# Batch normalization over 256 channels: half tiles in six buffers in place of whole tiles in three

## The chip, the cores and the metric

The kernel runs on one core of one Trainium2 chip. The metric is the time of one execution on the device, in microseconds; less is better. A DMA here is a transfer between the chip's main memory (DRAM) and the core's on-chip memory of 128 partitions. The core has 16 DMA engines; the SP engine issues the loads on one hardware queue, the ScalarE (ACT) engine the stores on another, and every transfer of 128 rows is spread over all 16 DMA engines.

## The reference

The input x has 32 images of 256 channels of 128 x 128 numbers (float32, 537 MB). Every channel gets one scale and one shift:

```
mean = running_mean.reshape(1, -1, 1, 1)
var = running_var.reshape(1, -1, 1, 1)
gamma = gamma.reshape(1, -1, 1, 1)
beta = beta.reshape(1, -1, 1, 1)
return gamma * (x - mean) / np.sqrt(var + eps) + beta
```

Each number is read once, gets a multiplication and an addition, and is written once: 1074 MB in both directions.

## The kernel before

A tile is one image and one block of 128 channels: 128 partitions by 16,384 columns (`HW`), 8 MB. There are 64 of them (`NT`), taken in `order`: all images of the first channel block, then of the second. Three buffers `t0` to `t2` are used in turn; the work is done in place.

SP issues the loads. Ahead of everything it issues half of tile 0 (L87), the four parameter rows (L90), the other half of tile 0 (L94) and tiles 1 and 2 (L96), with no wait between the tiles. After that, load i (L103) waits for two things: that store i-3 has emptied its buffer (L102), and that VectorE (DVE) has done the first part of tile i-1, which it does as soon as load i-1 has landed (L104, the semaphore `vdone`). So one load is in flight at a time.

DVE works out scale and shift per channel (L106 to L124), and then does two instructions a tile (`vector_part`, L127): columns 0 to `STEP` (2560), then `STEP` to `VCOLS` (14,336), or to `VLAST` (9216) in the last tile. Tile 0 is cut at its middle instead, since it is loaded in two halves. ACT does the rest of the columns (`scalar_part`, L138) once both DVE parts are done, and waits there for the store of tile i-1 to have landed (L164); then it issues the store of tile i (L153). So one store is in flight at a time. In the last tile ACT waits for neither DVE nor the store before, and only its store waits for both parts.

`loaded{s}` and `stored{s}` are semaphores for each buffer; a transfer adds 16, one from each DMA engine. There is no scheduler: each engine runs its instructions in the order that the code writes them.

Of the kernel before, what the change touches and what calls it, by code (L numbers as in the profile page):

```python
# [6 lines left out]


NBUF = 3
PAD = 936  # L10


STEP = 2560
VCOLS = 14336
VLAST = 9216


@with_exitstack
def kernel(
    ctx: ExitStack,  # L20
    tc: tile.TileContext,
    x: bass.AP,
    gamma: bass.AP,
    beta: bass.AP,
    running_mean: bass.AP,
    running_var: bass.AP,
    out: bass.AP,
):
    nc = tc.nc
    eps = 1e-5  # L30
    f32 = mybir.dt.float32

    N, C, H, W = x.shape
    P = nc.NUM_PARTITIONS
    assert C % P == 0
    NCB = C // P
    HW = H * W
    NT = N * NCB
    B = 32
    NQ = P // B  # L40
    NE = 16
    NPAR = 4

    xr = x.rearrange("n (cb p) h w -> (n cb) p (h w)", p=P)
    outr = out.rearrange("n (cb p) h w -> (n cb) p (h w)", p=P)

    def tile_of(name, *shape):
        return nc.alloc_sbuf_tensor(name, list(shape), f32)

    rows = tile_of("rows", B, NPAR * C)  # L50
    turned = tile_of("turned", B, NPAR * C)
    par = tile_of("par", P, NPAR, NCB)
    eps_t = tile_of("eps_t", P, 1)
    std_t = tile_of("std_t", P, NCB)
    rstd_t = tile_of("rstd_t", P, NCB)
    scale_t = tile_of("scale_t", P, NCB)
    ms_t = tile_of("ms_t", P, NCB)
    shift_t = tile_of("shift_t", P, NCB)
    tile_of("pad", P, PAD)
    bufs = [tile_of(f"t{s}", P, HW) for s in range(NBUF)]  # L60

    names = [f"loaded{s}" for s in range(NBUF)] + [f"stored{s}" for s in range(NBUF)]
    names += ["early", "vdone", "adone", "fetched", "vec", "act"]
    sems = {name: nc.alloc_semaphore(name) for name in names}
    loaded = [sems[f"loaded{s}"] for s in range(NBUF)]
    stored = [sems[f"stored{s}"] for s in range(NBUF)]
    early, vdone, adone, fetched, vec, act = (sems[n] for n in names[2 * NBUF :])
    used = range(min(s.num for s in sems.values()), max(s.num for s in sems.values()) + 1)
    assert len(used) == len(sems)

    count = [0]

    def step(inst, sem=None, value=None):
        if sem is not None:
            inst._wait_ge(sem, value)
        elif count[0]:
            inst._wait_ge(vec, count[0])
        inst.then_inc(vec, 1)
        count[0] += 1
        return count[0]  # L80

    left, right = slice(0, HW // 2), slice(HW // 2, HW)
    last = NT - 1
    order = [n * NCB + cb for cb in range(NCB) for n in range(N)]

    with tc.tile_critical():  # L86
        nc.sync.dma_start(out=bufs[0][:, left], in_=xr[order[0]][:, left]).then_inc(early, 16)  # L87
        zeroed = step(nc.vector.memset(rows[:], 0.0))  # L88
        for r, ap in enumerate((running_var, gamma, beta, running_mean)):
            inst = nc.sync.dma_start(out=rows[0:NE, r * C : (r + 1) * C], in_=ap.partition_broadcast(NE))  # L90
            if r == 0:
                inst._wait_ge(vec, zeroed)
            inst.then_inc(fetched, 16)
        nc.sync.dma_start(out=bufs[0][:, right], in_=xr[order[0]][:, right]).then_inc(loaded[0], 16)  # L94
        for i in range(1, NBUF):
            nc.sync.dma_start(out=bufs[i][:], in_=xr[order[i]]).then_inc(loaded[i], 16)  # L96
    tc.close()
    tc.compile()  # L98

    for i in range(NBUF, NT):  # L100
        s, turn = i % NBUF, i // NBUF
        nc.sync.wait_ge(stored[s], 16 * turn)  # L102
        inst = nc.sync.dma_start(out=bufs[s][:], in_=xr[order[i]]).then_inc(loaded[s], 16)  # L103
        inst._wait_ge(vdone, 2 * (i - 1) + 1)  # L104

    step(nc.vector.memset(eps_t[:], eps))  # L106
    step(nc.vector.transpose(out=turned[:], in_=rows[:]), fetched, 16 * NPAR)  # L107

    blocks = turned[:].rearrange("p (rc q b) -> p rc q b", q=NQ, b=B)
    flat = par[:].rearrange("p r cb -> p (r cb)")  # L110
    for q in range(NQ):
        placed = step(nc.vector.tensor_copy(out=flat[q * B : (q + 1) * B], in_=blocks[:, :, q, 0]))  # L112
    var_t, gamma_t, beta_t, mean_t = (par[:, r] for r in range(NPAR))
    nc.scalar.activation(  # L114
        out=std_t[:],
        in_=var_t,
        func=mybir.ActivationFunctionType.Sqrt,
        bias=eps_t[:],
        scale=1.0,
    )._wait_ge(vec, placed).then_inc(act, 1)  # L120
    step(nc.vector.reciprocal(out=rstd_t[:], in_=std_t[:]), act, 1)  # L121
    step(nc.vector.tensor_mul(out=scale_t[:], in0=gamma_t, in1=rstd_t[:]))  # L122
    step(nc.vector.tensor_mul(out=ms_t[:], in0=mean_t, in1=scale_t[:]))  # L123
    ready = step(nc.vector.tensor_sub(out=shift_t[:], in0=beta_t, in1=ms_t[:]))  # L124
    nc.vector.wait_ge(vec, ready)

    def vector_part(i, first, end):  # L127
        t, cb = bufs[i % NBUF], order[i] % NCB
        return nc.vector.tensor_scalar(  # L129
            out=t[:, first:end],  # L130
            in0=t[:, first:end],
            scalar1=scale_t[:, cb : cb + 1],
            scalar2=shift_t[:, cb : cb + 1],
            op0=mybir.AluOpType.mult,
            op1=mybir.AluOpType.add,
        ).then_inc(vdone, 1)

    def scalar_part(i, first):  # L138
        t, cb = bufs[i % NBUF], order[i] % NCB
        return nc.scalar.activation(  # L140
            out=t[:, first:],
            in_=t[:, first:],
            func=mybir.ActivationFunctionType.Identity,
            bias=shift_t[:, cb : cb + 1],
            scale=scale_t[:, cb : cb + 1],
        ).then_inc(adone, 1)

    def landed(i):
        return loaded[i % NBUF], 16 * (i // NBUF + 1)

    def store(i):
        s = i % NBUF
        nc.scalar.dma_start(out=outr[order[i]], in_=bufs[s][:])._wait_ge(adone, i + 1).then_inc(stored[s], 16)  # L153

    vector_part(0, 0, HW // 2)._wait_ge(early, 16)
    vector_part(0, HW // 2, VCOLS)._wait_ge(*landed(0))
    for i in range(1, NT):
        vector_part(i, 0, STEP)._wait_ge(*landed(i))
        vector_part(i, STEP, VLAST if i == last else VCOLS)
    for i in range(last):  # L160
        nc.scalar.wait_ge(vdone, 2 * (i + 1))
        inst = scalar_part(i, VCOLS)
        if i:
            inst._wait_ge(stored[(i - 1) % NBUF], 16 * ((i - 1) // NBUF + 1))  # L164
        store(i)
    scalar_part(last, VLAST)._wait_ge(*landed(last))
    nc.scalar.wait_ge(vdone, 2 * NT)
    store(last)

    for s in range(NBUF):  # L170
        nc.sync.wait_ge(stored[s], 16 * ((NT - s + NBUF - 1) // NBUF))
    nc.sync.sem_clear(used)
# [30 lines left out]
```

## Time and profile before

| | |
|---|---|
| Time, median of 3 runs | 2481.03 us (2480.61 to 2481.18) |
| The profiled execution | 2480.81 us, span 2479.5 us |
| Moved | 1073.85 MB, mean 433 GB/s |
| Load of 8 MB, issue to landing (median) | 37.0 us |
| Store of 8 MB, issue to landing (median) | 36.5 us |
| DVE `tensor_scalar`, all | 505.2 us in 128 instructions |
| ACT `activation` on tiles, all | 138.2 us in 64 instructions |

A line of the timeline has the start in the span, the duration, the engine and line, the operation with its tiles and shapes, and in brackets how long the engine was idle before it and what ended that. A line of the waits has the waiting engine and line, what it waited for, the total in us, how many times, and the longest. A line on a DMA queue has its packets, its MB, and the time of its packets as a share of 16 engines' span. The row of digits is the span in 40 equal slices, in tenths of busy time. SPq and ACTq are the parts of SP and ACT that issue transfers.

### The profile page before, as it was taken

To read this page: it belongs to the slowest core of one execution; us is meant where nothing else is said; L and a number is where in the kernel's file an instruction comes from. 1 tells how busy PE (TensorE), PEld (TensorE's weight loads), DVE (VectorE), ACT (ScalarE), POOL (GpSimd) and SP (SyncE) were. 2 spreads that over 40 slices of the span, in tenths; PEclk is the share of its full clock that TensorE was granted. 3 is DMA by queue.
4 is the path that set the end of the run, shared out by engine and by line. 5 is a ranking of instruction groups with operands and counts; after the bars stand their busy time and mean duration, and the time that the engine had idled before them with its cause. 6 is when DMAs were issued, how large, how long until landed. Compare 5 with 4: busy or idle time off the path is not lost.

```text
span 2479.5 us, 514 instructions
## 1 busy us (share of the span) xinstructions
DVE 508.7 (21%) x139; ACT 139.8 (6%) x66; POOL 0.2 (0%) x4
## 2 busy tenths in 40 slices
DVE  2122121221212212122121221212212122121220
ACT  0000000000000000000000000000000000000001
POOL 0000000000000000000000000000000000000000
DMA  9999999999999999999999999999999999999999
GB/s 412 435 438 427 437 438 429 436 438 429 435 438 430 435 439 430 433 438 433 431 438 432 432 438 432 432 438 432 432 438 433 431 438 433 431 438 435 430 438 410
DMA packets 18708, 1073.85 MB, mean 433 GB/s; under 512 B 2128, under 2 KB 2192, under 8 KB 2192
## 3 DMA queue, kind: packets, MB, share of 16 engines
q1 hardware_dynamic: 9488, 536.94, 50.1%
q10 hardware_dynamic: 9216, 536.88, 50.0%
q14 instruction: 4, 0.03, 0.0%
HBM read 536.94 MB, written 536.87 MB: 433 GB/s over the span
## 4 chain that ended last, share of the span: by engine, by line
DMA 92%; DVE 4%; another core or an unknown queue 2%; ACT 0%; issue 0%; SPq 0%; DVEq 0%
DMA t<-in_x_dram 92%; DVE t L129 4%; ACT t L140 0%; SPq L90 0%; DVE rows L88 0%; DVEq L98 0%; SPq L86 0%
## 5 line engine op out<-in xcount | busy, mean ns | idle before, releaser
L129 DVE TENSOR_SCALAR t<-t,scale_t,shift_t 128x11776 f32<-128x11776 f32 (+2 forms) x128 | 505.2, 3989 | 1928.4 <-DMA t<-in_x_dram 1928.3
L140 ACT ACTIVATE t<-t,shift_t,scale_t 128x2048 f32<-128x2048 f32 x64 | 138.2, 2159 | 2297.3 <-DMA out_dram<-t 2274.5
L107 DVE STREAM_TRANSPOSE turned<-rows 32x1024 f32<-32x1024 f32 x1 | 1.2, 1232 | 7.6 <-DMA rows<-in_running_mean_dram 7.6
L114 ACT ACT_TABLE_LOAD x1 | 1.3, 1283 | 6.4 <-PEq L98 6.4
L88 DVE MEMSET rows<- 32x1024 f32 x1 | 0.9, 912 | 1.2 <-SPq L86 1.2
L106 DVE MEMSET eps_t<- 128x1 f32 x1 | 0.1, 59 | 4.4 <-PEq L98 4.4
L114 ACT ACTIVATE std_t<-par,eps_t 128x2 f32<-128x2 f32 x1 | 0.3, 295 | 8.5 <-DVE par L112 8.5
L112 DVE COPY par<-turned 32x8 f32<-32x8 f32 x4 | 0.7, 162 | 0.1
L121 DVE RECIPROCAL rstd_t<-std_t 128x2 f32<-128x2 f32 x1 | 0.2, 165 | 0.4 <-ACT std_t L114 0.4
L122 DVE TENSOR_TENSOR scale_t<-par,rstd_t 128x2 f32<-128x2 f32 x1 | 0.2, 161 | 0.0
L123 DVE TENSOR_TENSOR ms_t<-par,scale_t 128x2 f32<-128x2 f32 x1 | 0.2, 161 | 0.0
L124 DVE TENSOR_TENSOR shift_t<-par,ms_t 128x2 f32<-128x2 f32 x1 | 0.2, 160 | 0.0
L187 POOL MEMSET const-bfloat16-1.0<- 128x1 bf16 x1 | 0.1, 101 | 0.0
L187 POOL MEMSET const-uint8-127<- 128x1 uint8 x1 | 0.1, 101 | 0.0
L187 POOL MEMSET const-float32-0.0<- 128x1 f32 x1 | 0.1, 98 | 0.2 <-issue 0.2
L187 POOL MEMSET const-float32-1.0<- 128x1 f32 x1 | 0.1, 98 | 0.0
## 6 DMA issues: line engine op xcount, KB each, us to landing
t<-in_x_dram SPq DMA_DIRECT2D x2, 4096.0 KB, 16.0
out_dram<-t ACTq DMA_DIRECT2D x64, 36.5
t<-in_x_dram SPq DMA_DIRECT2D x63, 37.0
rows<-in_running_var_dram SPq DMA_DIRECT2D x1, 16.0 KB, 11.2
rows<-in_gamma_dram SPq DMA_DIRECT2D x1, 16.0 KB, 11.0
rows<-in_beta_dram SPq DMA_DIRECT2D x1, 16.0 KB, 10.7
rows<-in_running_mean_dram SPq DMA_DIRECT2D x1, 16.0 KB, 10.7
```

Of the source, the lines that this page charges most:

```text
L88: zeroed = step(nc.vector.memset(rows[:], 0.0))
L106: step(nc.vector.memset(eps_t[:], eps))
L107: step(nc.vector.transpose(out=turned[:], in_=rows[:]), fetched, 16 * NPAR)
L112: placed = step(nc.vector.tensor_copy(out=flat[q * B : (q + 1) * B], in_=blocks[:, :, q, 0]))
L114: nc.scalar.activation(out=std_t[:], in_=var_t, func=mybir.ActivationFunctionType.Sqrt, bias=eps_t[:], scale=1.0,)._wait_ge(vec, placed).t ...
L121: step(nc.vector.reciprocal(out=rstd_t[:], in_=std_t[:]), act, 1)
L122: step(nc.vector.tensor_mul(out=scale_t[:], in0=gamma_t, in1=rstd_t[:]))
L123: step(nc.vector.tensor_mul(out=ms_t[:], in0=mean_t, in1=scale_t[:]))
L124: ready = step(nc.vector.tensor_sub(out=shift_t[:], in0=beta_t, in1=ms_t[:]))
L129: return nc.vector.tensor_scalar(out=t[:, first:end], in0=t[:, first:end], scalar1=scale_t[:, cb : cb + 1], scalar2=shift_t[:, cb : cb + 1 ...
L140: return nc.scalar.activation(out=t[:, first:], in_=t[:, first:], func=mybir.ActivationFunctionType.Identity, bias=shift_t[:, cb : cb + 1] ...
L187: nc = _bacc.Bacc("TRN2", target_bir_lowering=False, num_devices=1)
```

## The change

Each tile is cut into two halves by columns (`SPLIT = 2`), and each half is a tile of its own, 128 x 8192, 4 MB, with its own load, its own work and its own store. There are 128 of them, and six buffers of half the size, so the on-chip memory used is the same. `VCOLS` and `VLAST` are halved; `STEP` stays at 2560. The rules of waiting are the same lines with the new index: load i waits for store i-6 and for the first DVE part of half tile i-1; ACT's part of half tile i waits for the store of half tile i-1. Six loads are issued without a wait between them at the start, the first of them ahead of the parameter rows. The special cut of tile 0 and its semaphore `early` go, since a half tile is what it was cut into. The two halves of one image and block follow each other, so the rows of a transfer are 32,768 bytes out of 65,536.

```
-NBUF = 3
+SPLIT = 2
+NBUF = 3 * SPLIT
...
-VCOLS = 14336
-VLAST = 9216
+VCOLS = 7168
+VLAST = 4608
...
+    COLS = HW // SPLIT
+    NT = N * NCB * SPLIT
...
-    bufs = [tile_of(f"t{s}", P, HW) for s in range(NBUF)]
+    bufs = [tile_of(f"t{s}", P, COLS) for s in range(NBUF)]
...
-    order = [n * NCB + cb for cb in range(NCB) for n in range(N)]
+    order = [(n, cb, h) for cb in range(NCB) for n in range(N) for h in range(SPLIT)]
+
+    def part_of(ap, i):
+        n, cb, h = order[i]
+        return ap[n * NCB + cb][:, h * COLS : (h + 1) * COLS]
+
+    def load(i):
+        s = i % NBUF
+        return nc.sync.dma_start(out=bufs[s][:], in_=part_of(xr, i)).then_inc(loaded[s], 16)
...
-        nc.sync.dma_start(out=bufs[0][:, left], in_=xr[order[0]][:, left]).then_inc(early, 16)
+        load(0)
...
-        nc.sync.dma_start(out=bufs[0][:, right], in_=xr[order[0]][:, right]).then_inc(loaded[0], 16)
         for i in range(1, NBUF):
-            nc.sync.dma_start(out=bufs[i][:], in_=xr[order[i]]).then_inc(loaded[i], 16)
+            load(i)
...
     for i in range(NBUF, NT):
-        s, turn = i % NBUF, i // NBUF
-        nc.sync.wait_ge(stored[s], 16 * turn)
-        inst = nc.sync.dma_start(out=bufs[s][:], in_=xr[order[i]]).then_inc(loaded[s], 16)
-        inst._wait_ge(vdone, 2 * (i - 1) + 1)
+        s = i % NBUF
+        nc.sync.wait_ge(stored[s], 16 * (i // NBUF))
+        load(i)._wait_ge(vdone, 2 * (i - 1) + 1)
...
     def store(i):
         s = i % NBUF
-        nc.scalar.dma_start(out=outr[order[i]], in_=bufs[s][:])._wait_ge(adone, i + 1).then_inc(stored[s], 16)
+        nc.scalar.dma_start(out=part_of(outr, i), in_=bufs[s][:])._wait_ge(adone, i + 1).then_inc(stored[s], 16)
 
-    vector_part(0, 0, HW // 2)._wait_ge(early, 16)
-    vector_part(0, HW // 2, VCOLS)._wait_ge(*landed(0))
-    for i in range(1, NT):
+    for i in range(NT):
         vector_part(i, 0, STEP)._wait_ge(*landed(i))
         vector_part(i, STEP, VLAST if i == last else VCOLS)
```

## The prediction

> **What bounds the kernel now.** I read the page first (engines, DMA, chain), then the waits, then the middle of the chain and of the timeline, then the packet records of the trace.
>
> ```profile
> DVE 508.7 (21%) x139; ACT 139.8 (6%) x66; POOL 0.2 (0%) x4
> DMA  9999999999999999999999999999999999999999
> q1 hardware_dynamic: 9488, 536.94, 50.1%
> q10 hardware_dynamic: 9216, 536.88, 50.0%
> DMA 92%; DVE 4%; another core or an unknown queue 2%; ACT 0%; issue 0%; SPq 0%; DVEq 0%
> ```
> The engines compute a quarter of the time, the DMA engines are busy in every slice. Queue 1 is the loads, queue 10 the stores: 9216 packets are 64 stores of 144, namely 128 rows of 65,536 bytes and 16 four-byte marks that count up the semaphore, so each of the 16 DMA engines moves 8 rows a store.
>
> ```profile
> SPq L102 <- DMA out_dram<-t: 1395.0, 61, 66.0
> SPq L103 <- DVE t L129: 984.8, 61, 16.5
> ...
> ACT t L140 <- DMA out_dram<-t: 2274.5, 62, 43.3
> ```
> A load waits last (16.1 us a time) for vector work on the load before it; a store waits for the store before it (36.7 us through its ACT part). Neither queue ever holds a second transfer in the steady part.
>
> ```profile
> 1208.96 7.93 DVE L129 TENSOR_SCALAR t<-t,scale_t,shift_t 128x2560 f32<-128x2560 f32 x2 [30.70 <-DMA t<-in_x_dram]
> 1210.59 77.61 SPq L103 DMA_DIRECT2D t<-in_x_dram  x3
> 1233.09 2.09 ACT L140 ACTIVATE t<-t,shift_t,scale_t 128x2048 f32<-128x2048 f32 x1 [36.57 <-DMA out_dram<-t]
> 1235.21 0.34 ACTq L153 DMA_DIRECT2D out_dram<-t  x1
> 1247.60 7.93 DVE L129 TENSOR_SCALAR t<-t,scale_t,shift_t 128x2560 f32<-128x2560 f32 x2 [30.71 <-DMA t<-in_x_dram]
> ```
> One tile takes 38.64 us (1208.96 to 1247.60). A load lands, DVE does 2560 columns, the next load is issued 1.63 us later; half a period on, a store lands, ACT does 2048 columns, the next store is issued 2.12 us later. The chain of waits counts those 1.62 us of DVE, but the DMA engines do not stop there. In the packet records 65,536-byte packets follow each other every 2.4141 us on each engine, 16 of them and two marks make the 38.64 us, and no engine has an idle microsecond from 1.95 us to its end at 2476.6 to 2479.0. So the bound is bytes: 64 loads and 64 stores of 8 rows are 1024 packets per engine, 2472 us.
>
> The order of packets matters for the change. On the engine that finishes last, a period reads (L load, S store, dot a mark) `L . L L L S L S . S S S L S L S L`: two transfers take turns, and while one queue is empty the other runs alone for 4 packets (5 or 6 on engines that are ahead). From the mark of a load to the next load being ready at the engines is 3.03 us: 0.35 to landing, 0.03, 1.62 of DVE, 0.04, and about 1.0 from issue (also the 1.0 between the first issue at 0.95 us and the first packet at 1.95). A newly ready queue is taken one whole packet late, and a mark costs its queue a turn. For stores the same sum with 2.09 us of ACT is 3.5 us.
>
> **The change, part by part.** Tiles of 8192 columns, 128 loads and 128 stores, six buffers.
>
> (1) Rows of 32,768 bytes. Only the first tile has such packets now. Seven steps of one engine there, between 14 and 22 us, take 8.466 us, so 1.2094 each, 2.4189 a pair against 2.4141: 4.7 ns on 1016 rows per engine = **+4.8 us**. They are loads running alone; mixed with stores they are not seen. With 65,536 bytes loads and stores cost the same, alone or mixed, so I take the load's price; the ends are 0 (half of 2.4141) and, for a loss, twice it, 9.6.
>
> (2) Marks: 256 transfers in place of 129, 6 ns each on the path: **+0.8 us**.
>
> (3) DVE and ACT. Per half tile DVE does 2560 columns (1.62) and 4608: the 8192- and 6144-column rows (4.55 and 3.48) give 0.52 ns a column and 0.27 fixed, so 2.7 us; ACT does 1024 columns: 2048 took 2.09 and 7168 took 6.36, so 0.83 ns a column and 0.38 fixed, 1.24 us. In a 19.36 us period both fit behind the DMA: 0. The 122 loads on SP (0.43 us an issue) likewise.
>
> (4) The pauses of a queue, now twice as many, against a cover half as long. STEP stays 2560, so a load still needs 3.03 us from mark to ready; a store now 0.33+0.03+1.24+0.03+1.03 = 2.66. In slots of 1.209 us these are 2.5 and 2.2. Rounded up to a boundary, plus the late packet, plus the mark's turn: the other queue must run alone for 5 packets of its 8. Five fit twice into 16, so a period without idle exists: 16 x 1.2094 + 0.01 = 19.36 us. Which phase the two queues fall into is decided at the start, so I count it.
>
> Tile 0 is ready for DVE at 17.46 as before (end of the parameter chain), its DVE parts end at 21.8, ACT at 23.0, store 0 is issued at 23.07 and ready at 24.1. Loads 1 to 5 are queued; load 2 starts at 22.3 to 23.1, so 3 of its packets pass before the first S. Then, with a mark taking a turn at each end of a load: 8 S among 8 load turns, 4 further L, 8 S among 8 load turns, 4 further L, and store 2 begins with 7 packets of load 5 left. Both therefore run out together, after 56 packets, near 92 us; load 6 could not be queued before load 5 landed (L103's rule). Then the engines idle. Store 3 is ready after 2.66 us, load 6 after 3.03; the store gets 2 packets alone, so ends 2 packets before the load, whose remainder covers part of its pause; next idle 1.45 us, 3 alone; next 0.24 us, 4 alone; then none, since three packets after the mark (3.6 us) cover 2.66. Idle once: 2.66+1.45+0.24 = **+4.4 us**, and three restarts (the first full packets behind the parameter rows, at 12.3 us, took 1.52 us, 0.3 over) **+0.7**, a part of their 0.9 lying behind the other queue. Bounds: 0, if the store's first pause slips by a packet, and 7.
>
> (5) The end. Now the engines end over 2.4 us, one packet; with halves over 1.2: **-0.6** (0 to -1.2). The last tile now has 3584 columns on ACT, 3.4 us; store 126 runs 9.7 us meanwhile: 0. Without that cover it would cost 3.4+1.1.
>
> Sum: the profiled execution took 2480.8 (span 2479.5 and 1.3 around it), +4.8+0.8+4.4+0.7-0.6 = 2490.9; the median is 0.2 above that execution: **2491 us**, +0.4%.
>
> The Trainium skill, "DMA: Bandwidth & Descriptors", section "Anatomy of one DMA — SWDGE (gpsimd) path", gives each transfer a fixed 2 us beside its bytes (for the other kind of queue). Added on the path, 127 further transfers would be an estimated 254 us, 2735 in all. Here the pause is as long, but lies behind the other queue; whether it still does is the first rival. The same page, "Queues, rings and completion order", lets an engine drain a whole packet of some 9 to 17 descriptors before it changes queue; the trace shows it changing after every row, and the measurement decides. By the page 8 rows of a store would cover a load's pause at once, no idle, and the sum would be 2486.
>
> **The rivals.**
> (a) The pauses lock on top of each other. If load 6 is ready before store 3, the load gets 2 packets alone, the store then ends 2 packets after it; the load's mark comes after one of them, the load is ready 2.5 slots later: 1.5 slots = 1.8 us idle, and then again 2 packets alone. Nothing moves it, as the load's pause (2.5 slots) is the longer one. 122 x 1.83 = 223 us: 2709. With 3 packets 0.6 us, 76 us: 2562. For it: I forecast ready times only 0.37 us apart, the engines are 0.9 us apart at load 2, and reads stalled by up to 1.2 us when the first store came. It decides from 0.37 us the other way. Against: both queues end on the same last engine, which favours the store. That a new transfer is taken one packet late could also be a fixed 2.4 us, which the trace cannot tell apart; then 0 to 0.6 us a period.
> (b) Not slower. The half row costs half of 2.4141 once stores are between, and load 6 comes in time: 2480.8+0.8-0.6+0.2 = 2481. For it: 1.2094 is from a stretch that held the first packets of the run. Against: the steps there are even to the nanosecond. It decides from 1.207 us a packet.
> (c) No idle at the start, (1) and (2) as said: 2486. For it: the trace of before has none there.
>
> **How the numbers follow.** My forecast 0.52 (own range 2487 to 2495); (a) 0.28; (c) 0.12; (b) 0.08. The limit of 0.2%, about what a measurement can tell from no change, is 5 us, 2486.0. (a) and the forecast lie above, (c) on it, (b) below; a gain of 5 us would need a faster packet than any in the trace: 0.03. Slower 0.87, within 0.10, faster 0.03. Range: from 2484, between (b) and (c), to 2620, which takes in the 3-packet lock with restarts (76 and 122 x 0.4 = 49, some 2611) and leaves out the 2-packet one.
>
> **What would show it.** Landings of loads 19.36 us apart in the middle, and a store landing some 3.6 us ahead of each load; the DMA share under 9 only near 92 to 130 us; L103's analogue ending the loads' waits. A period of 20 to 21.5 us with the load landing 1 to 2 us before the store would show (a). A 32,768-byte packet at 1.207 us would put (1) at 0. The forecast is wrong if loads and stores fall into step.

## The result, and the profile after

The changed kernel takes 2759.9 us (median of 4 runs, 2751.1 to 2776.0), the kernel before 2480.9: a ratio of 1.113, 95% interval 1.1105 to 1.1156. The forecast was 2491, with a range of 2484 to 2620.

The page of the profile after (2756.5 us, span 2755.2), parts 1 to 4:

```profile
DVE 540.0 (20%) x267; ACT 162.5 (6%) x130; POOL 0.2 (0%) x4
...
DMA  9999999999999999999999999999999999999998
...
q1 hardware_dynamic: 18560, 536.94, 51.5%
q10 hardware_dynamic: 18432, 536.88, 45.1%
...
DMA 93%; ACT 6%; DVE 0%; issue 0%; SPq 0%; ACTq 0%; DVEq 0%
```

The compute engines are as idle as before. What is new is in the two queue lines. Loads (q1) and stores (q10) move the same bytes, and before the change both took 50% of the DMA engines' time. Now the loads' packets take 6.4% of 2755 us more than the stores': 176 us. And the two shares add up to 96.6%: the other 3.4%, 94 us, is idle DMA. The packet records give the same two terms more closely, per DMA engine: 176 us by which packets of loads took longer than 1.213 us each, and 99 us without a packet. Together they make up the 275.7 us that the span grew by, to within a few us. (Before: some 2 us and less than 1 us.) The row of digits shows nothing of this: a slice is 69 us long, and a long packet counts as busy.

The timeline of after in its middle (start, duration, engine and line, operation, idle before):

```profile
1195.29 4.20 DVE L136 TENSOR_SCALAR t<-t,scale_t,shift_t 128x2560 f32<-128x2560 f32 x2 [17.68 <-DMA t<-in_x_dram]
1196.93 43.81 SPq L93 DMA_DIRECT2D t<-in_x_dram  x3
1198.88 1.24 ACT L147 ACTIVATE t<-t,shift_t,scale_t 128x1024 f32<-128x1024 f32 x1 [20.65 <-DMA out_dram<-t]
1200.15 0.34 ACTq L160 DMA_DIRECT2D out_dram<-t  x1
1216.68 4.20 DVE L136 TENSOR_SCALAR t<-t,scale_t,shift_t 128x2560 f32<-128x2560 f32 x2 [17.19 <-DMA t<-in_x_dram]
```

A DVE line starts when a load has landed, an ACT line when a store has. The period here is 21.4 us (1195.29 to 1216.68), not 19.36; over the middle four fifths of the run it is 21.5. And a store lands 3.6 us after a load, a sixth of a period; before the change it landed 24.1 us after a load, in a period of 38.6. So the two queues stand differently to each other. The packet records of one engine in a typical period (L and S a packet of a load or store, a dot a mark), and the long packets with their start and duration in us:

```
before   LLLLLS.SSSSSLSLSL.     loads alone, stores alone, taking turns
after    LLLLLSLSLSLS.SSSS.     loads alone, taking turns, stores alone
after    1198.50 L 1.63   1200.13 L 1.22   1201.35 L 1.75   1203.09 L 1.64   1204.73 S 1.21
```

In the order of after, an engine passes straight from stores alone to loads alone. Nearly all of the long packets lie in that stretch of loads (some 171 of the 176 us): the first is mostly 1.3 to 2.2 us, the last before the next store 1.2 to 2.0, and a third of those between them are long too. Of the packets of loads that take turns with stores, 98 in 100 are 1.21 again. The long ones differ from engine to engine, so the engines spread: the last marks of the load that landed at 1195.29 came between 1192.2 and 1194.9 us. A transfer has landed when the slowest engine is done, and the next is issued only then, so the faster engines run out of work. In 58 of 100 passages from stores alone to loads alone the engine was idle before the first load.

### The profile page after: what moved, and what is told of

Read it like the earlier page. It is cut to its first block, busy times and chain, and to the rows that moved or that the text cites. A ratio compares the mean times of both kernels' runs of the same rounds, so it can differ in the third digit from the quotient of the medians.

```text
span 2755.2 us, 960 instructions
## 1 busy us (share of the span) xinstructions
DVE 540.0 (20%) x267; ACT 162.5 (6%) x130; POOL 0.2 (0%) x4
## 4 chain that ended last, share of the span: by engine, by line
DMA 93%; ACT 6%; DVE 0%; issue 0%; SPq 0%; ACTq 0%; DVEq 0%
DMA out_dram<-t 92%; ACT t L147 6%; DMA rows<-in_running_mean_dram 0%; DVE t L136 0%; DVE turned L114 0%; SPq L99 0%; DVE rows L97 0%; DVE par L119 0%; ACTq L160 0%; ACT std_t L121 0%; DVE rstd_t L128 0%; DVE shift_t L131 0%; DVE ms_t L130 0%; DVE scale_t L129 0%; DVEq L106 0%
## 5 line engine op out<-in xcount | busy, mean ns | idle before, releaser
L136 DVE TENSOR_SCALAR t<-t,scale_t,shift_t 128x2560 f32<-128x2560 f32 (+2 forms) x256 | 536.5, 2138 | 2166.2 <-DMA t<-in_x_dram 2166.1
L147 ACT ACTIVATE t<-t,shift_t,scale_t 128x1024 f32<-128x1024 f32 x128 | 160.9, 1257 | 2560.7 <-DMA out_dram<-t 2555.2
```

The costliest lines, as they stand in the source:

```text
L136: return nc.vector.tensor_scalar(out=t[:, first:end], in0=t[:, first:end], scalar1=scale_t[:, cb : cb + 1], scalar2=shift_t[:, cb : cb + 1 ...
L147: return nc.scalar.activation(out=t[:, first:], in_=t[:, first:], func=mybir.ActivationFunctionType.Identity, bias=shift_t[:, cb : cb + 1] ...
```

## The experiments

The first four tested theory P (the pauses of the queues fall on top of each other) against R (short rows are read slowly).

**Two loads in flight.** Half tiles, load i waits for DVE on half tile i-2.

```
-        load(i)._wait_ge(vdone, 2 * (i - 1) + 1)
+        load(i)._wait_ge(vdone, 2 * (i - 2) + 1)
```

> Half tiles as changed, but load i waits for the first DVE part of half tile i-2, so two loads may be in flight and the load queue has no pause. Theory P (the pauses of the two queues fall into step and then neither covers the other; the 99 us of idle and the 176 us of long reads per engine both follow from that): 2484 to 2492 us. Rival R (rows of 32,768 bytes are read slowly beside stores, whatever the pacing): the 176 us of long reads stay, 2640 or more.

Measured 2928.3 us, ratio 1.180 (1.178 to 1.182): slower still. P's forecast fell; R's came by its numbers (2640 or more, and the long reads stay), but the waits give another reason for the time. The DMA queue's own wait in this run (line, waited for, us, times, longest), that of ACT, and its queue lines:

```profile
SPq L110 <- DMA out_dram<-t: 2739.0, 121, 39.6
```
```profile
ACT t L147 <- DMA out_dram<-t: 2730.2, 126, 24.2
```
```profile
q1 hardware_dynamic: 18560, 536.94, 48.9%
q10 hardware_dynamic: 18432, 536.88, 42.4%
```

L110 is the wait for an empty buffer. Freed of the pacing, the loads ran ahead until all six buffers were full, and from then on each load was released by a store's landing, which also releases the next store: both queues are empty at the same moment, every half tile. Idle is 259 us per engine here, long reads 191.

**Two stores in flight.** ACT's part of half tile i waits for store i-2.

```
-        if i:
-            inst._wait_ge(stored[(i - 1) % NBUF], 16 * ((i - 1) // NBUF + 1))
+        if i > 1:
+            inst._wait_ge(stored[(i - 2) % NBUF], 16 * ((i - 2) // NBUF + 1))
```

> Half tiles as changed, but ACT's part of half tile i waits for store i-2, so two stores may be in flight and the store queue has no pause; loads one at a time as in the change. P: 2484 to 2492, since one queue without a pause is enough. R: 2640 or more. If long reads come only while loads run alone, none should be left here, as loads never run alone.

Measured 2762.6 us, ratio 1.114 (1.112 to 1.116), as the change itself. Its waits:

```profile
ACT t L147 <- DVE t L136: 2501.7, 124, 23.9
```
```profile
SPq L93 <- DVE t L136: 2629.1, 122, 53.6
```

The mirror image: now the stores run ahead until they have nothing left to store, and ACT waits for the half tile that has just been loaded. A load's landing releases both queues. My expectation that one queue without a pause is enough missed that a queue without a rule of its own runs into the other one. Long reads are still there (170 us), so P's forecast fell again and R's came by its numbers; with both queues waiting for the same landing this run is no test of either. Loads did run alone here (the records read `SSSSS.LLLLSLSLSLSLSSSS.`), so the third forecast was not put to the test.

**Half transfers, paced by whole tiles.**

```
-        load(i)._wait_ge(vdone, 2 * (i - 1) + 1)
+        inst = load(i)
+        if i % SPLIT == 0:
+            inst._wait_ge(vdone, 2 * (i - 1) + 1)
...
-        if i:
+        if i and i % SPLIT == 0:
             inst._wait_ge(stored[(i - 1) % NBUF], 16 * ((i - 1) // NBUF + 1))
```

> Half tiles with rows of 32,768 bytes and six buffers, but the rules of pacing per whole tile again: two half loads are issued one behind the other when the second half of the pair before has landed, and two half stores in the same way. Only the size of the transfers is changed against the kernel before. P: as before plus the price of shorter packets and more marks, 2484 to 2490. R: 2640 or more.

Measured 2618.7 us in the middle of four runs that vary, 2565 to 2653; the ratio of 1.041 (1.032 to 1.049) is that of the two shortest, 2565.0 and 2599.6. In the profiled run idle is 13 us but long reads 70: between the theories. The records show how: 100 us into the run loads and stores take turns both behind the loads alone and behind the stores alone (`LLLLLS.SLSLSLSLSLSLSL.LS.SSSSSLSLSL.`), and nearly every packet takes 1.21 us; after 200 us eight stores alone are followed by eight to ten loads alone, as in the change, and many of the first and last of these loads are long (mostly up to 2.0 and 2.1 us), most of those between them 1.21. So the same rows are short or long within one run, which speaks against R.

**Whole tiles with longer pauses.**

```
-VCOLS = 14336
+VCOLS = 10240
...
-        inst._wait_ge(vdone, 2 * (i - 1) + 1)
+        inst._wait_ge(vdone, 2 * i)
```

> Whole tiles as before, with longer pauses: a load waits for both DVE parts of the tile before it, and ACT does 6144 columns (VCOLS 10240). The pause of a load from mark to ready is 7.3 us by the rows of before, that of a store 6.9, in packets about 3 and 2.9 of 2.414 us, as the change has 2.5 and 2.2 of 1.209. P, if only the ratio of pause to transfer counts: slower, by 62 times 1 to 4 us, 2540 to 2730. R: 2481, as the rows are whole. If the start decides the phase, 2481 too.

Measured 2739.0 us in one run (before: 2481.8). Its queue lines:

```profile
q1 hardware_dynamic: 9488, 536.94, 49.3%
q10 hardware_dynamic: 9216, 536.88, 45.2%
```

Rows of 65,536 bytes show the same signature: 110 us of long reads, 151 us of idle. R is out. The other two forecasts fell as well, P's by 9 us, and the 2481 that was to hold if the start decides. The rate by slices of 68 us, and ACT's main wait:

```profile
GB/s 415 429 443 429 411 386 369 412 370 383 398 383 396 370 404 377 383 398 382 399 380 386 383 383 398 380 401 377 389 383 383 398 383 398 376 379 396 380 398 398
```
```profile
ACT t L140 <- DVE t L129: 2012.9, 54, 38.2
```

For some 300 us this run has the rate and the order of before (1.6 us lost between 100 and 300 us); then the order turns into that of after, and some 10 us are lost in each 100. So the start does not fix the order for good: the longer pauses moved it. In most tiles ACT waits for DVE, so that a load's landing releases both queues, as in the second experiment. What remained was the order in which an engine's packets come, and that the start has a part in setting it. The next experiments tested this theory O against S (twice the pauses with half the cover cost this much in any order).

**Four loads at the start in place of six.** Loads 4 and 5 wait for the half tile before them; the steady rules are untouched.

```
-        for i in range(1, NBUF):
+        for i in range(1, 4):
             load(i)
...
-    for i in range(NBUF, NT):
+    for i in range(4, NT):
         s = i % NBUF
-        nc.sync.wait_ge(stored[s], 16 * (i // NBUF))
+        if i >= NBUF:
+            nc.sync.wait_ge(stored[s], 16 * (i // NBUF))
```

> The changed kernel, but only four half loads are issued without a wait at the start; loads 4 and 5 already wait for the half tile before them. Nothing else differs. Theory O (the order decides: before, an engine goes from loads alone to stores alone to taking turns; changed, from stores alone to loads alone to taking turns, and in that order reads are long, engines spread and idle follows; the start sets the order): by counting packets from the changed kernel's records, load 4 then starts while store 1 is alone and ends as store 2 starts, the order of before; 2484 to 2500. Rival S (twice as many pauses with half the cover cost this much in any order): 2700 or more.

Measured 2491.7 us (2488.2 to 2508.9), ratio 1.0047 (1.002 to 1.0074). Queue lines and middle of the timeline:

```profile
q1 hardware_dynamic: 18560, 536.94, 50.0%
q10 hardware_dynamic: 18432, 536.88, 50.0%
```
```profile
1197.87 4.21 DVE L137 TENSOR_SCALAR t<-t,scale_t,shift_t 128x2560 f32<-128x2560 f32 x2 [15.64 <-DMA t<-in_x_dram]
...
1209.66 1.24 ACT L148 ACTIVATE t<-t,shift_t,scale_t 128x1024 f32<-128x1024 f32 x1 [18.30 <-DMA out_dram<-t]
...
1216.94 4.20 DVE L137 TENSOR_SCALAR t<-t,scale_t,shift_t 128x2560 f32<-128x2560 f32 x2 [14.86 <-DMA t<-in_x_dram]
```

The store lands 11.8 us after a load in a period of 19.1 here, over half a period as before the change, and the records read `LLLLLS.SSSSSLSLSL`, the order of before. Long reads are 3.6 us, long packets of stores 3.1, idle 6. As many transfers, pauses and short rows as in the change, and 268 us less: S is out.

**Pairs of stores together.** The third experiment, with one more edit that makes store 0 start later:

```
-        store(i)
+        if i % SPLIT:
+            store(i - 1)
+            store(i)
     scalar_part(last, VLAST)._wait_ge(*landed(last))
     nc.scalar.wait_ge(vdone, 2 * NT)
+    store(last - 1)
     store(last)
```

> e3 (half transfers, pacing per whole tile), but both stores of a pair are issued when both halves are done, so that store 0 starts about as late as in the kernel before. Rows of 32,768 bytes and the number of transfers stay. O: the start is that of before, so the order of before, and what is left is the price of packets and marks: 2484 to 2490. S, or a price of short rows beside stores: 2560 or more as e3.

Measured 2489.4 us (2489.2 to 2489.7), ratio 1.0028 (1.0018 to 1.0039). Long reads 1.9 us, idle 6. The order is a third one, `LL.LLLLSLSLSLS.SSS.SSSLSLSLSLSLSL`: between stores alone and loads alone they always take turns. So the time came as forecast and the order did not. This is the price of half transfers by themselves: the period of two halves is 2 x 19.369 us against 38.637, so 0.10 us in each of 64 tiles, 6.5 us.

**A shorter pause.** `STEP = 512` in the changed kernel.

> The changed kernel with STEP 512 in place of 2560, so a load's pause is 1.1 us shorter (3.0 to 1.9) and the first DVE part 0.5 us. O: a load is ready earlier, but the order is set at the start; the engines idle less, the long reads stay: 2640 to 2740. S, if the length of the pause decides: idle and long reads both go, 2486 to 2520.

Measured 2574.5 us, ratio 1.037 (1.035 to 1.039), below the range of O and above that of S. Queue lines:

```profile
q10 hardware_dynamic: 18432, 536.88, 51.2%
q1 hardware_dynamic: 18560, 536.94, 48.7%
```

Here the stores' packets are the long ones, 72 us, and the loads' are not (7 us); idle is 10. The order has become `.LLLL.SSSSSLSLSLSL`: a store becomes ready just as the engine runs out of load packets, and in 58 of 100 such passages its first packet is long, mostly 1.9 to 2.2 us; most of the others are 1.21. So the pause does move the order, which I had put down to the start alone, and a transfer that starts just as an engine runs out of work can pay for it in its first packet.

**Whole tiles, store 0 late.** One wait added to the kernel before, at the first store:

```
+        if i == 0:
+            nc.scalar.wait_ge(vdone, 3)
         store(i)
```

> The kernel before, whole tiles, with one wait added: ACT issues store 0 only after DVE's first part of tile 1, some 28 us later than before. Everything else as before. O: tile 2 has landed when store 0 starts, the loads then wait for buffers, so a load starts as a store ends, the order of the changed kernel: more than the 28 us of the late start, 2550 to 2750, with long reads and idle in the steady part. S: whole tiles cover their pauses in any order, at most 2481 plus the late start, 2510.

Measured 2724.7 us, ratio 1.0975 (1.0953 to 1.0997). The DMA queue's own waits and the queue lines:

```profile
SPq L102 <- DMA out_dram<-t: 2605.4, 61, 75.3
```
```profile
q1 hardware_dynamic: 9488, 536.94, 49.2%
q10 hardware_dynamic: 9216, 536.88, 45.5%
```

Tile 1 lands sooner without a store beside it, so store 0 is issued at 44.4 us and not at 29.1, 15 us late and not 28. That costs 243 us. Every load now waits for a buffer (L102, as in the first experiment), a period is 42.6 us, with 98 us of long reads and 145 us of idle in all. Nothing about the tiles had changed.

**Three and five loads at the start.** The edit of four, with 3 and 5.

> The changed kernel with three half loads issued without a wait at the start (six in the change, four in e5). O, by counting packets with a newly ready queue taken two half packets late: load 3 is ready while store 0 has three packets left and starts as store 0 ends, so the order is that of the change: 2680 to 2780. If fewer loads at the start are better as such, it is as e5: 2486 to 2510.

> Five half loads issued without a wait at the start. O, by the same count: load 4 ends a packet after store 1, both queues are empty for some 1.5 us, store 2 is ready first and gets four packets alone, after which a store starts as a load ends, the order of before: 2486 to 2510. If more loads at the start are worse as such, it lies between e5 and the change, 2550 to 2700.

Measured 2791.4 us (ratio 1.124, 1.118 to 1.130) for three and 2510.9 us (1.011, 1.008 to 1.015) for five. Both went the way of the count, a little above its ranges. The queue lines of three:

```profile
q1 hardware_dynamic: 18560, 536.94, 51.4%
q10 hardware_dynamic: 18432, 536.88, 44.7%
```

| Loads at the start | 3 | 4 | 5 | 6 (the change) |
|---|---|---|---|---|
| us | 2791.4 | 2491.7 | 2510.9 | 2759.9 |
| Long packets, us per engine | 189 | 7 | 19 | 176 |
| Idle, us per engine | 115 | 6 | 8 | 99 |

With three the order is `LLLLLSLSLSLS.SSSS.` as in the change, with five that of before, with up to eight packets alone on the engines that are ahead; after some 600 us most engines run eight loads alone and eight stores alone with hardly a turn between (`LLLLLLLL.SSSSSSSS.`), and lose little by it. With four this comes after 1600 us. Neither "fewer is better" nor "more is better" makes this row.

## Why the prediction was wrong

**What bounds the kernel** was read rightly: packets without a gap on all 16 engines, and no other engine near.

**(1) and (2)**, shorter packets and more marks: forecast 5.6 us, measured 6.5 in the pairs with their stores together. **(3)** holds: a half tile takes DVE 4.20 us (forecast 4.3) and ACT 1.24. The chain of after has ACT at 6%, as a part of each store's pause; with four loads at the start it has 7%, and hardly anything is lost by it there.

**(4)** is the step that failed, in two places. The length of the pauses was right: the marks of the load that landed at 1195.29 were done by 1194.87, and the next load's packets start at 1197.91, 3.04 us later (forecast 3.03). But "a newly ready queue is taken one whole packet late" does not carry over to half packets. Store 1 was issued at 48.39 us, ready at 49.4, and its packets began at 52.3 to 52.8 on 15 of the 16 engines, two half packets and a part late. It is the 2.4 us that I named under rival (a) as the other reading and did not count with. Reads stalled at the first store, too, so on most engines four packets of load 2 passed it and not three. Counted again so, load 6 starts as store 2 ends, and in the records it does, at 91.0 to 91.6 us on 15 of the 16 engines. The idle of 4.4 us never came (0.8 us between 85 and 130); in its place came the order of after.

The second place is the sentence behind it: "Five fit twice into 16, so a period without idle exists: 19.36 us. Which phase the two queues fall into is decided at the start". The first half is true, and so is the second for the change, whose order held; the conclusion that any such phase is free was wrong. The experiment with four loads shows one at 19.41 us; the change fell into another, which by the count has no idle either, and there the reads grow by 1.4 us a half tile and idle by 0.8. Before the change the long reads come to some 2 us in the whole run, most of it in the first 150 us, since its phase avoids them; I took the packet's duration for a property of the packet.

**Rival (a)** had the right place and size (2709) with 0.28, but not the mechanism: it lost 1.8 us a half tile to a ready time that comes too late, with two packets alone. The records show five alone, and most of the loss in long packets. The sign that I gave, a period of 20 to 21.5 us, was close; "the load landing 1 to 2 us before the store" was 3.6. My own forecast had the store landing 3.6 us ahead of the load; that the number came, the other way round, is chance. **Rival (c)** had the time of the other order (2486 against 2489 and 2492 measured) for another reason. **(b)** fell with the 6.5 us of (1) and (2). The range left out the part of (a) that came.

**The fixed cost of a transfer.** The Trainium skill's 2 us a transfer ("DMA: Bandwidth & Descriptors", "Anatomy of one DMA — SWDGE (gpsimd) path") made an estimated 2735 us, close to the result. The runs do not bear out the rule as the cause: with the same 256 transfers, four loads at the start and pairs of stores cost 10 and 7.5 us. A pause that is not the kernel's own work is there: of the 3.04 us above, 1.64 lie between the start of DVE's part and the next issue (1195.29 to 1196.93), and the other 1.4 do not. Whether the pause is hidden differs with the order.

**(5)**, the end, is too small beside the rest to be read from these runs.

**Open.** Why an engine's load packets are long after stores alone was not settled. It is not the row size, nor loads running alone as such, nor a store becoming ready as such: the sixth experiment has these at 1.21 us. Nor is it the passage from stores alone to loads alone as such: with four and five loads at the start there are 560 and 1289 such passages with no idle time before them, and in 99 of 100 the first load takes 1.21 us. What differs is that there the load is ready before the stores run out: the engine was idle before the load in at most 1 of 100 passages, and in the change in 58. In the change the first load is long in 95 of 100 passages with idle time before it, and in 70 of 100 without, so that idle time is not all of it. So the start decides the loss, which the runs with three to six loads and with store 0 late show, and the order goes with it; that the order is the cause by itself, and not a load that is ready too late, is not shown. Whether it needs all 16 engines to make the passage together was not tried.

## What to carry to other kernels

With one load and one store at a time, ask how the two stand to each other, and not only whether each pause fits behind the other transfer; the first few transfers have a large part in setting it. In the kernel before, in the change and with whole tiles and store 0 late it then held for the whole run; in the third and fourth experiments it turned within some 300 us. So a changed tile size has to be measured with several numbers of loads at the start before it is judged: here that number alone is worth 300 us. And a rule that holds one queue back can be what keeps it from running into the other; taking it away made both queues wait for the same landing.

## What the runs showed of the hardware that was not expected

- A packet of 32,768 bytes of a load takes 1.213 us while loads and stores take turns. In the change, where an engine passes from stores alone to loads alone, the first load takes mostly 1.3 to 2.2 us and the last before the next store 1.2 to 2.0; the store's packets stay at 1.213. Rows of 65,536 bytes do the same (98 and 110 us of long reads in all). With four and five loads at the start the same passage has its first load at 1.21 us in 99 of 100.
- A load that becomes ready (1.0 us after its issue) while stores run is served some 2.4 us later or more with rows of both sizes, in the kernel before and with four and five loads at the start. For stores it is 2.5 us or more before and 2.9 in the change, but down to 0.7 with four loads and 0.4 with five, so it is no fixed time.
- A transfer that starts just as an engine runs out of work can have a longer first packet: mostly 1.9 to 2.2 us in place of 1.21 for 58 of 100 stores with the shorter pause.
- Times scatter more in some of these kernels: 2751 to 2776 us for the change, 2565 to 2653 for the third experiment and 2488 to 2509 with four loads at the start, against 2480.6 to 2481.2 for the kernel before beside the change. The order of after does not do it by itself: two loads in flight took 2927 to 2932.
